# Up-projections as three 256-column products per weight block, with the modulated input moved 32 bytes against the weights

## The chip, the core and the metric

One core of a Trainium2 chip runs the whole kernel as one launch. The metric is the device time in microseconds. Three runs of the kernel before have a median of 2254.69 us (2251.78 to 2254.91). One more execution was taken by the hardware profiler; it took 2256.46 us, and its instructions span 2254.7 us.

## The reference

A trunk of two decoder layers over one sequence of 256 tokens, width 2048, all in float32. Layer 0 mixes tokens with a forgetting attention (16 heads of 128), layer 1 with a sliding-window attention (32 query heads of 64 in 4 groups, window 128, learned sinks). Each mixer is followed by a gated ConvFFN of inner width 5632. A conditioning vector `c` gives shift, scale and gate of every sub-layer:

```
c_act = silu(c)
for i in range(2):
    mod = c_act @ ada_w[i] + ada_b[i]                 # 2048 x 12288
    sh1, sc1, g1, sh2, sc2, g2 = split(mod, 6)
    h = x * (1 + sc1) + sh1
    y = attention_i(h)                                # fox_w_in / swa_w_in, then w_o
    x = layer_norm(ALPHA * x + (1 + g1) * y)
    h = x * (1 + sc2) + sh2
    u = h @ ffn_w_up[i]                               # 2048 x 11264
    u = u[s-2]*w0 + u[s-1]*w1 + u[s]*w2 + conv_b      # causal, along the tokens
    g, val = split(u, 2)
    y = (silu(g) * val) @ ffn_w_down[i]               # 5632 x 2048
    x = layer_norm(ALPHA * x + (1 + g2) * y)
```

## The kernel before, in words

**Products in three parts.** The large matrix products run on TensorE in the fp32r format. To keep float32 accuracy each operand is split into a high part (the value rounded to fp32r) and a low part (what is left). A product is then high·high + high·low + low·high, added up in PSUM. `stream` (L256 on) walks over a weight matrix in blocks of 256 rows by 512 columns: one DMA from the SP queue brings a block `w` (512 KB), ScalarE writes its high part `wh` (L264), VectorE its low part `wl` (L275), and then the block's products are issued by the function that the caller gave. `w` has 10 buffers, `wh` and `wl` 4 each. Every matmul instruction loads its own stationary operand (128 x 128) first.

**The modulated input.** `h` of a sub-layer lies transposed in SBUF, for each of 16 chunks of 128 features the 256 tokens of the high part and, right behind them, the 256 tokens of the low part. This is the tile `hHL`, [128, 16, 2, 256]; `hH` and `hL` are views of it.

**Two kinds of product.** Where the input is stationary and the weights move (`x_mm`, tiles named `xs`), each instruction has 512 moving columns. This is used for the value projections, the sliding-window layer's projections, both output projections and the down-projection, whose stationary operand is the gated activation `gT`. Where the weights are stationary (`w_mm`, tiles `ws`), each instruction moves 256 tokens; the q and k projections of layer 0 do this, in three products per 128 x 128 weight piece. The up-projections have a form of their own, `u_mm` (tiles `us`): two products per weight piece. The first moves all 512 columns of a chunk of `hHL` over the high weights, which leaves high·high in one half of a PSUM bank and low·high in the other; the second moves the 256 columns of `hH` over the low weights, into the first half.

**The up-projection pass.** `conv_ffn` splits the inner width into two parts (6 and 5 blocks of 512 columns). For each block it makes two passes of `w_stationary`, one for the gate half and one for the value half, each over all 16 chunks (8 weight blocks); then the down-projection of that part follows. A pass fills four banks of the eight in PSUM. What follows a pass is deferred: `evac` is a generator of which a step is run before each later weight block's products. Its `conv` adds the two halves of a bank (ScalarE copies the second half to SBUF at L1071, VectorE adds it at L1073), then does the convolution along the tokens (L1075 on ScalarE, L1076 and L1078 on VectorE).

**Work in the gaps.** The conditioning products (`ada_w`, 201 MB) run on VectorE as multiply-adds (L404), fed at a rate per weight block that `ada.update` sets. All pools are rings; the order on each engine is that of the program as the tile framework's scheduler lays it.

**Where tiles lie.** In the built program `hHL` starts at a multiple of 256 bytes in each partition. The weight buffers (`w`, `wh`, `wl`) and the general tiles of pool `gp` (`gT`, `oT`, `qh`, `kT`, `A`, ...) all start at 224 bytes beyond a multiple of 256.

Of the kernel before, what the change touches and what calls it, by code (L numbers as in the profile page):

```python
# [10 lines left out]
F32 = mybir.dt.float32  # L11
F32R = mybir.dt.float32r
I32 = mybir.dt.int32
AF = mybir.ActivationFunctionType
ALU = mybir.AluOpType
AX = mybir.AxisListType

P = 128
D = 2048
S = 256  # L20
NT = S // P
KC = D // P
# [19 lines left out]
def hybrid_trunk(ctx: ExitStack, tc: tile.TileContext, a: dict, out: bass.AP):  # L42
    nc = tc.nc
# [4 lines left out]
    cst = ctx.enter_context(tc.tile_pool(name="cst", bufs=1))  # L48
# [3 lines left out]
    tp = ctx.enter_context(tc.tile_pool(name="tp", bufs=4))  # L52
# [3 lines left out]
    def wtile(name="w"):  # L56
        return wp.tile([P, 2, WB], F32, tag="w", name=name)

    def gtile(name="g"):
        return gp.tile([P, 2, S], F32R, tag="g", name=name)  # L60

    def ttile(name="t"):
        return tp.tile([P, 2 * S], F32, tag="t", name=name)

    def bank(name="sm"):
        return psp.tile([P, 512], F32, tag="ps", name=name)

    def w_banks():
        return [bank("ws").rearrange("p (a s) -> p a s", a=2) for _ in range(2)]
# [4 lines left out]
    def mm(o, lhsT, rhs, start=False, stop=False, **kw):  # L74
        return nc.tensor.matmul(o, lhsT, rhs, start=start, stop=stop, **kw)  # L75

    def pin(ins, on=True):

        if on:
            tc.keep_in_program_order(ins)  # L80

    def split(h, l, src):

        nc.scalar.copy(h, src)  # L84
        nc.vector.tensor_tensor(l, src, f32(h), op=ALU.subtract)
# [125 lines left out]
    def then(fn, alone=False):  # L211

        if alone:
            lone.add(fn)
        work.append(fn)
        if len(work) == 1 and not ahead[0]:
            settle()
# [3 lines left out]
    def settle(left=0):  # L221
        while work and (ahead[0] > left or not left):
            f = work.pop(0)
            rest(f, *work)
            f()
# [17 lines left out]
    def defer(gen):  # L243

        post.append(gen)

    def run_post():
        for g in list(post):
            if next(g, post) is post:
                post.remove(g)  # L250
# [5 lines left out]
    def stream(wsrc, row0, col, ks, use):  # L256

        for kc in ks[::2]:
            r0 = (row0 + kc) * P
            w = wtile()  # L260
            pin(nc.sync.dma_start(w, wsrc[r0:r0 + 2 * P, col:col + WB].rearrange("(k p) f -> p k f", p=P)), False)
            h = hl.tile([P, 2, WB], F32R, tag="wh", name="wh")
            l = hl.tile([P, 2, WB], F32R, tag="wl", name="wl")
            pin(nc.scalar.copy(h, w), False)  # L264

            def go(kc=kc, h=h, l=l):
                ahead[0] -= 1
                run_post()
                use(kc, h, l)
                if feeds:  # L270
                    feeds.pop(0)()
                tick()

            def residual_(w=w, h=h, l=l, go=go):
                pin(nc.vector.tensor_tensor(l, w, f32(h), op=ALU.subtract), behind[0] > 0)  # L275
                behind[0] -= 1
                del residuals[go]

            ahead[0] += 1
            weights.add(go)  # L280
            residuals[go] = residual_
            work.append(go)
            settle(2)
# [25 lines left out]
    def w_mm(ps, kc, h, l, last=KC - 1, first=0):  # L309

        for i in range(2):
            for f in range(4):
                o = ps[f // 2][:, f % 2, :]
                wh, wl = h[:, i, f * P:(f + 1) * P], l[:, i, f * P:(f + 1) * P]
                mm(o, wh, hH[:, kc + i, :], start=kc + i == first and f % 2 == 0, skip_group_check=True)
                mm(o, wh, hL[:, kc + i, :], skip_group_check=True)
                mm(o, wl, hH[:, kc + i, :], stop=kc + i == last, skip_group_check=True)

    def u_banks():
        return [bank("us").rearrange("p (a s) -> p a s", a=2) for _ in range(4)]  # L320

    def u_mm(ps, kc, h, l):

        for f in range(4):
            for i in range(2):
                wh, wl = h[:, i, f * P:(f + 1) * P], l[:, i, f * P:(f + 1) * P]
                mm(ps[f], wh, hHL[:, kc + i], start=kc + i == 0, skip_group_check=True)
                mm(ps[f][:, 0, :], wl, hH[:, kc + i, :], stop=kc + i == KC - 1, skip_group_check=True)

    def x_stationary(wsrc, col, k0, nk, stat, end=0):  # L330

        ps = x_banks()
        use = x_mm_end(ps, stat, nk, end) if end else lambda kc, h, l: x_mm(ps, kc, h, l, stat, nk - 1)
        stream(wsrc, k0, col, list(range(nk)), use)
        return ps

    def w_stationary(wsrc, col):

        ps = u_banks()
        stream(wsrc, 0, col, list(range(KC)), lambda kc, h, l: u_mm(ps, kc, h, l))  # L340
        return ps


# [22 lines left out]
    def tick():  # L366
        ada_tick()
        if not feeds:
            step()
# [110 lines left out]
            ada_step()  # L480


    hHL = cst.tile([P, KC, 2, S], F32R, name="hHL")
    hH, hL = hHL[:, :, 0, :], hHL[:, :, 1, :]

    def mod_turn(k, n=1):

# [576 lines left out]
    def conv_ffn(l):  # L1064
        w_up, w_dn = a["ffn_w_up"][l], a["ffn_w_down"][l]
        NB = DFF // WB
        cw = lambda j, f: ccol[:, l, j, f:f + 1]

        def conv(pf, f):
            c = tp.tile([P, S], F32, tag="c", bufs=2, name="c")  # L1070
            nc.scalar.copy(c, pf[:, 1, :])  # L1071
            pf = pf[:, 0, :]
            nc.vector.tensor_tensor(pf, pf, c, op=ALU.add)  # L1073
            u = tp.tile([P, S], F32, tag="u", bufs=3, name="u")
            nc.scalar.activation(u, pf, AF.Identity, bias=cw(CW, f), scale=cw(2, f))  # L1075
            nc.vector.scalar_tensor_tensor(u[:, 1:], pf[:, :S - 1], cw(1, f), u[:, 1:],  # L1076
                                           op0=ALU.mult, op1=ALU.add)
            nc.vector.scalar_tensor_tensor(u[:, 2:], pf[:, :S - 2], cw(0, f), u[:, 2:],  # L1078
                                           op0=ALU.mult, op1=ALU.add)
            return u  # L1080

        def evac(ps, f0, then):
            u = None
            for f in range(5):
                v = conv(ps[f], f0 + f) if f < 4 else None
                if u is not None:
                    then(f - 1, u)
                u = v
                yield

        def silu(sil):
            def f_(f, u):
                nc.scalar.activation(sil[f // 2][:, (f % 2) * S:(f % 2 + 1) * S], u, AF.Silu)
            return f_

        def gated(sil, gT):
            def f_(f, u):
                nc.vector.tensor_tensor(u, u, sil[f // 2][:, (f % 2) * S:(f % 2 + 1) * S], op=ALU.mult)
                g = gtile("gT")
                split(g[:, 0, :], g[:, 1, :], u)  # L1100
                gT.append(g)
            return f_

        sbs = [(0, 6), (6, NB)]
        for si, (b0, b1) in enumerate(sbs):
            gT = []
            then(lambda: ada.update(rate=(0.64, 0.4)[l]))
            for b in range(b0, b1):
                ps = w_stationary(w_up, b * WB)
                sil = [ttile("sil") for _ in range(2)]  # L1110
                then(lambda ps=ps, b=b, sil=sil: defer(evac(ps, b * 4, silu(sil))))
                ps = w_stationary(w_up, DFF + b * WB)
                then(lambda ps=ps, b=b, sil=sil, gT=gT: defer(evac(ps, DFF // P + b * 4, gated(sil, gT))))

            def stat(kc, t, gT=gT):
                while kc >= len(gT):
                    run_post()
                return gT[kc][:, 0, t * P:(t + 1) * P], gT[kc][:, 1, t * P:(t + 1) * P]

            def ready(si=si):  # L1120
                if si == 0:
                    drain()
                ada_need(l, 5)
                ada["rate"] = (0.78, 0.4)[l]

            then(ready)
            for d in range(D // WB):
                ps = x_stationary(w_dn, d * WB, b0 * 4, (b1 - b0) * 4, stat, (2, 4)[l] if si > 0 and d == D // WB - 1 else 0)
                then(lambda ps=ps, d=d, si=si: defer(residual(ps, d, gates[l, 5], si == len(sbs) - 1)),
                     si > 0 and d == D // WB - 1)  # L1130
        then(lambda: (flush(), ada.update(gate_free=True)), True)
# [26 lines left out]
    for t in range(NT):  # L1158
        mu, rs, _ = moments[t]
        for d in range(D // 512):  # L1160
            c = slice(d * 512, (d + 1) * 512)
# [29 lines left out]
```

## Time and profile before

| What | Before |
|---|---|
| median of 3 runs | 2254.69 us (2251.78 to 2254.91) |
| profiled execution: its time, its span | 2256.46 us, 2254.7 us |
| TensorE matmul busy | 2203.7 us (98%), 12087 instructions recorded |
| TensorE weight load busy | 1908.6 us (85%) |
| VectorE busy | 1847.5 us (82%) |
| ScalarE busy | 1209.7 us (54%) |
| HBM | 602.66 MB, 267 GB/s on average |
| up-projection stages | 481 to 759, 892 to 1117, 1506 to 1780 and 1910 to 2132 us |

How to read it: matmuls are pipelined and the end of each is modelled, so the "busy" time of one (393 ns for a 512-column product) is longer than the step from its start to the next one's start. The step is what counts, and it is read from the start column of the timeline. In the timeline "x2" means that two equal instructions in a row were merged into one line, which carries the start of the first.

### The profile page before, as it was taken

To read this page: it belongs to the slowest core of one execution; us is meant where nothing else is said; L and a number is where in the kernel's file an instruction comes from. 1 tells how busy PE (TensorE), PEld (TensorE's weight loads), DVE (VectorE), ACT (ScalarE), POOL (GpSimd) and SP (SyncE) were. 2 spreads that over 40 slices of the span, in tenths; PEclk is the share of its full clock that TensorE was granted. 3 is DMA by queue.
4 is the path that set the end of the run, shared out by engine and by line. 5 is a ranking of instruction groups with operands and counts; after the bars stand their busy time and mean duration, and the time that the engine had idled before them with its cause. 6 is when DMAs were issued, how large, how long until landed. Compare 5 with 4: busy or idle time off the path is not lost. (4 is left out here: it accounts for less than half of the span.)

```text
span 2254.7 us, 33120 instructions
## 1 busy us (share of the span) xinstructions
PE 2203.7 (98%) x12087; PEld 1908.6 (85%) x12087; DVE 1847.5 (82%) x2626; ACT 1209.7 (54%) x2009; POOL 22.8 (1%) x52
## 2 busy tenths in 40 slices
PE   6999999999999999999999999999999999999997
PEld 5999888788888888888887788788888888888886
DVE  6879999979989978799888899769988655676766
ACT  3435655455555543655634588746555533555542
POOL 0000000000000000000000000000000000000000
PEclk9999999999999999999999999999999999999999
DMA  9999999958978989889887777557887555565553
GB/s 336 371 336 364 349 357 325 329 200 298 327 266 296 315 299 339 272 277 319 280 309 284 244 246 243 206 185 262 289 270 256 190 192 195 189 193 189 188 195 112
DMA packets 274228, 602.66 MB, mean 267 GB/s; under 512 B 21062, under 2 KB 29960, under 8 KB 273552
## 3 DMA queue, kind: packets, MB, share of 16 engines
q1 hardware_dynamic: 273008, 595.85, 76.5%
q0 software_dynamic: 1056, 4.69, 0.6%
q8 instruction: 94, 1.54, 0.3%
q14 instruction: 70, 0.57, 0.1%
HBM read 598.37 MB, written 2.10 MB: 266 GB/s over the span
## 5 line engine op out<-in xcount | busy, mean ns | idle before, releaser
L264 ACT CAST wh<-w 128x1024 fp32r<-128x1024 f32 x728 | 763.8, 1051 | 806.4 <-PE us L75 284.5
L275 DVE TENSOR_TENSOR wl<-w,wh 128x1024 fp32r<-128x1024 f32 x728 | 887.2, 1223 | 297.0 <-ACT wh L264 285.1
L75 PE MATMUL us<-hHL,wh 128*128 128x512 f32 x2816 | 983.7, 393 | 0.0
L75 PE MATMUL us<-hHL,wl 128*128 128x256 f32 x2816 | 790.4, 282 | 3.0 <-DVE wl L275 3.0
L75 PEld LDWEIGHTS us<-hHL,wh 128*128 128x128 f32 x2816 | 528.9, 188 | 112.0 <-issue 2.5
L75 PEld LDWEIGHTS us<-hHL,wl 128*128 128x128 f32 x2816 | 533.0, 189 | 8.4 <-DVE wl L275 4.3
L75 PE MATMUL xs<-wh,gT 128*128 128x512 f32 x1408 | 435.5, 390 | 0.0
L75 PEld LDWEIGHTS xs<-wh,gT 128*128 128x128 f32 x1408 | 264.3, 188 | 54.6
L75 PE MATMUL xs<-wl,gT 128*128 128x512 f32 x704 | 273.9, 389 | 0.0
L75 PE MATMUL xs<-wh,hHL 128*128 128x512 f32 x704 | 237.6, 403 | 0.1
L404 DVE SCALAR_TENSOR_TENSOR acc<-wa,cact,acc 128x1024 f32<-128x1024 f32 x180 | 228.8, 1280 | 0.0
L75 PE MATMUL ws<-hHL,wh 128*128 128x256 f32 x1024 | 191.3, 289 | 4.4 <-ACT hHL L84 2.1
L75 PEld LDWEIGHTS ws<-hHL,wh 128*128 128x128 f32 x1024 | 163.1, 196 | 6.9 <-ACT hHL L84 2.3
L404 DVE SCALAR_TENSOR_TENSOR acc<-wa,cactp,acc 128x1024 f32<-128x1024 f32 x128 | 162.6, 1281 | 0.0
L75 PEld LDWEIGHTS xs<-wh,hHL 128*128 128x128 f32 x704 | 131.5, 189 | 29.4 <-issue 1.0
L75 PEld LDWEIGHTS xs<-wl,gT 128*128 128x128 f32 x704 | 132.2, 188 | 27.3
L75 PE MATMUL ws<-hHL,wl 128*128 128x256 f32 x512 | 144.7, 290 | 2.2 <-DVE wl L275 2.2
L75 PE MATMUL xs<-wl,hHL 128*128 128x512 f32 x352 | 140.6, 400 | 1.6 <-DVE wl L275 1.5
L75 PE MATMUL xs<-wh,oT 128*128 128x512 f32 x384 | 124.6, 394 | 0.8 <-ACT wh L264 0.7
L1075 ACT ACTIVATE u<-us,ccol 128x256 f32<-128x256 f32 x176 | 98.0, 561 | 39.6 <-DVE us L1073 39.5
L75 PEld LDWEIGHTS ws<-hHL,wl 128*128 128x128 f32 x512 | 99.5, 197 | 2.8 <-DVE wl L275 2.8
L1076 DVE SCALAR_TENSOR_TENSOR u<-us,ccol,u 128x255 f32<-128x255 f32 x176 | 83.6, 480 | 13.2 <-ACT u L1075 12.9
(222 smaller groups left out, 1761.2 us busy)
## 6 DMA issues: line engine op xcount, KB each, us to landing
w<-in_ffn_w_up_dram SPq DMA_DIRECT2D x352, 512.0 KB, 4.6
wa<-in_ada_w_dram SPq DMA_DIRECT2D x320, 512.0 KB, 5.4
w<-in_ffn_w_down_dram SPq DMA_DIRECT2D x176, 512.0 KB, 4.1
w<-in_fox_w_in_dram SPq DMA_DIRECT2D x96, 512.0 KB, 7.0
wo<-in_ada_w_dram SPq DMA_DIRECT2D x48, 512.0 KB, 8.4
w<-in_swa_w_in_dram SPq DMA_DIRECT2D x40, 512.0 KB, 5.0
w<-in_fox_w_o_dram SPq DMA_DIRECT2D x32, 512.0 KB, 6.2
w<-in_swa_w_o_dram SPq DMA_DIRECT2D x32, 512.0 KB, 4.7
```

The costliest lines, as they stand in the source:

```text
L75: return nc.tensor.matmul(o, lhsT, rhs, start=start, stop=stop, **kw)
L264: pin(nc.scalar.copy(h, w), False)
L275: pin(nc.vector.tensor_tensor(l, w, f32(h), op=ALU.subtract), behind[0] > 0)
L404: pin(nc.vector.scalar_tensor_tensor(ac, wo, (cactp if row else cact)[:, k:k + 1], ac, op0=ALU.mult, op1=ALU.add), True)
L1075: nc.scalar.activation(u, pf, AF.Identity, bias=cw(CW, f), scale=cw(2, f))
L1076: nc.vector.scalar_tensor_tensor(u[:, 1:], pf[:, :S - 1], cw(1, f), u[:, 1:], op0=ALU.mult, op1=ALU.add)
```

## The change

It has four parts. The up-projections use `w_mm`, as the q and k projections of layer 0 do: per weight piece three products of 256 columns, two banks per pass in place of four. `conv` therefore reads finished sums, and the copy and the add go (L1071 to L1074). `evac` takes two steps per 128 columns in place of one. And the modulated input becomes two planes, all of `hH` and then all of `hL`, in a tile with 64 elements to spare, starting 8 elements (32 bytes) into it; the DMA scratch area at the bottom of SBUF is cut from 4096 to 2048 bytes. In the built program the planes now start at 32 bytes beyond a multiple of 256, and the weight buffers and general tiles at 224 as before, so these lie 192 bytes (mod 256) above the modulated input where they lay 224 above it.

```
-    def u_banks():
-        return [bank("us").rearrange("p (a s) -> p a s", a=2) for _ in range(4)]
-
-    def u_mm(ps, kc, h, l):
-        for f in range(4):
-            for i in range(2):
-                wh, wl = h[:, i, f * P:(f + 1) * P], l[:, i, f * P:(f + 1) * P]
-                mm(ps[f], wh, hHL[:, kc + i], start=kc + i == 0, skip_group_check=True)
-                mm(ps[f][:, 0, :], wl, hH[:, kc + i, :], stop=kc + i == KC - 1, skip_group_check=True)
...
     def w_stationary(wsrc, col):
-        ps = u_banks()
-        stream(wsrc, 0, col, list(range(KC)), lambda kc, h, l: u_mm(ps, kc, h, l))
+        ps = w_banks()
+        stream(wsrc, 0, col, list(range(KC)), lambda kc, h, l: w_mm(ps, kc, h, l))
         return ps
...
-    hHL = cst.tile([P, KC, 2, S], F32R, name="hHL")
-    hH, hL = hHL[:, :, 0, :], hHL[:, :, 1, :]
+    hpad = cst.tile([P, 2 * KC * S + 64], F32R, name="hH")
+    hH, hL = (hpad[:, 8 + a * KC * S:8 + (a + 1) * KC * S].rearrange("p (k s) -> p k s", s=S) for a in range(2))
...
         def conv(pf, f):
-            c = tp.tile([P, S], F32, tag="c", bufs=2, name="c")
-            nc.scalar.copy(c, pf[:, 1, :])
-            pf = pf[:, 0, :]
-            nc.vector.tensor_tensor(pf, pf, c, op=ALU.add)
             u = tp.tile([P, S], F32, tag="u", bufs=3, name="u")
...
-                v = conv(ps[f], f0 + f) if f < 4 else None
+                v = conv(ps[f // 2][:, f % 2, :], f0 + f) if f < 4 else None
                 if u is not None:
                     then(f - 1, u)
                 u = v
                 yield
+                yield
...
-    nc = _bacc.Bacc("TRN2", target_bir_lowering=False, num_devices=1, dynamic_dma_scratch_size=4096)
+    nc = _bacc.Bacc("TRN2", target_bir_lowering=False, num_devices=1, dynamic_dma_scratch_size=2048)
```

The first place is TensorE in the first weight block of the first up-projection pass. The number behind a tile's name tells buffers apart: `us_4824` and `us_4825` are the first two of the pass's four PSUM banks. Before:

```order
L75 MATMUL us_4824<-hHL_127,wh_4830 128x512
L75 MATMUL us_4824<-hHL_127,wl_4831 128x256
L75 MATMUL us_4824<-hHL_127,wh_4830 128x512
L75 MATMUL us_4824<-hHL_127,wl_4831 128x256
L75 MATMUL us_4825<-hHL_127,wh_4830 128x512
L75 MATMUL us_4825<-hHL_127,wl_4831 128x256
L75 MATMUL us_4825<-hHL_127,wh_4830 128x512
L75 MATMUL us_4825<-hHL_127,wl_4831 128x256
```

In the changed program, at the same weight block (`ws_4824` and `ws_4825` are all the banks that the pass has):

```order
L75 MATMUL ws_4824<-hH_127,wh_4828 128x256 x2
L75 MATMUL ws_4824<-hH_127,wl_4829 128x256
L75 MATMUL ws_4825<-hH_127,wh_4828 128x256
L75 MATMUL ws_4825<-hH_127,wl_4829 128x256
L75 MATMUL ws_4825<-hH_127,wh_4828 128x256 x2
L75 MATMUL ws_4825<-hH_127,wl_4829 128x256
L75 MATMUL ws_4824<-hH_127,wh_4828 128x256 x2
```

Each pair of a 512- and a 256-column product has become three of 256, with the high weights loaded twice in a row. A pass adds into half banks, and the block's first 128 rows go over all four column pieces before its second 128 rows do, where before the two row halves of one column piece followed each other.

The second place is VectorE at the end of the same pass, where the first bank is evacuated (`wl` is a weight block's low part, `u` the convolution's result, `x` the residual stream, `acc` the sum of a conditioning vector). Before:

```order
L275 TENSOR_TENSOR wl<-w,wh 128x1024
L673 TENSOR_SCALAR x<-ln,x 128x512
L1073 TENSOR_TENSOR us<-us,c 128x256
L275 TENSOR_TENSOR wl<-w,wh 128x1024
L1076 TENSOR_SCALAR u<-us,ccol,u 128x255
L1073 TENSOR_TENSOR us<-us,c 128x256
L1078 TENSOR_SCALAR u<-us,ccol,u 128x254
L404 TENSOR_SCALAR acc<-wa,cactp,acc 128x1024
```

Now:

```order
L275 TENSOR_TENSOR wl<-w,wh 128x1024
L662 TENSOR_SCALAR x<-ln,x 128x512
L1061 TENSOR_SCALAR u<-ws,ccol,u 128x255
L275 TENSOR_TENSOR wl<-w,wh 128x1024
L1063 TENSOR_SCALAR u<-ws,ccol,u 128x254
L393 TENSOR_SCALAR acc<-wa,cactp,acc 128x1024
```

The adds are gone, and the low parts of the weights stand with fewer instructions between them (lines have moved up by 11 to 15).

## The prediction

> **What bounds the kernel now.** I read the page's head first, then the groups by form, then busy time by stage, TensorE's waits, and last the timeline, because only starts give a matmul's true step.
>
> ```profile
> span 2254.7 us, 33120 instructions
> PE 2203.7 (98%) x12087; PEld 1908.6 (85%) x12087; DVE 1847.5 (82%) x2626; ACT 1209.7 (54%) x2009; POOL 22.8 (1%) x52
> ```
>
> TensorE is busy throughout. By stage (engines' busy us, granted clock, DMA share, GB/s):
>
> ```profile
> 60.00:190.00 130.00, 128.72 (x898) 120.71 (x898) 107.50 (x109) 55.70 (x71) 2.58 (x5) 0.95 1.02 358
> 190.00:350.00 160.00, 154.58 (x1118) 142.78 (x1116) 150.89 (x212) 91.58 (x179) 5.85 (x12) 1.00 0.99 354
> 480.00:760.00 280.00, 277.02 (x1575) 241.97 (x1574) 259.77 (x362) 160.47 (x249) 0.00 (x0) 0.99 0.84 288
> 892.00:1117.00 225.00, 225.00 (x1310) 199.77 (x1309) 198.19 (x273) 133.20 (x240) 0.00 (x0) 1.00 0.85 289
> 1506.00:1780.00 274.00, 274.00 (x1571) 240.92 (x1570) 236.67 (x337) 158.46 (x247) 0.00 (x0) 1.00 0.77 255
> 1910.00:2132.00 222.00, 222.00 (x1281) 196.73 (x1281) 152.82 (x226) 123.26 (x190) 0.00 (x0) 1.00 0.59 190
> ```
>
> The last four rows are the up-projections, 1001 of 2255 us: TensorE never pauses there, while DMA (0.59 to 0.85) and VectorE have room, VectorE least in the first (259.77 of 280). From 60 to 350 us the DMA engines are full (1.02, 0.99), so weights' arrival limits that stretch as much as products do. TensorE's waits in an up-projection, over the whole span:
>
> ```profile
> PE us L75 <- DVE wl L275: 3.0, 3, 1.4
> ```
>
> So what a weight piece's products take decides. The groups (busy us, mean ns with a modelled end):
>
> ```profile
> L75 PE MATMUL us<-hHL,wh 128*128 128x512 f32 x2816 | 983.7, 393 | 0.0
> L75 PE MATMUL us<-hHL,wl 128*128 128x256 f32 x2816 | 790.4, 282 | 3.0 <-DVE wl L275 3.0
> L75 PE MATMUL ws<-hHL,wh 128*128 128x256 f32 x1024 | 191.3, 289 | 4.4 <-ACT hHL L84 2.1 <-ACT wh L264 1.3 <-ACT hHL L503 1.0
> L75 PE MATMUL ws<-hHL,wl 128*128 128x256 f32 x512 | 144.7, 290 | 2.2 <-DVE wl L275 2.2
> L75 PE MATMUL xs<-wh,hHL 128*128 128x512 f32 x704 | 237.6, 403 | 0.1
> L75 PE MATMUL xs<-wl,hHL 128*128 128x512 f32 x352 | 140.6, 400 | 1.6 <-DVE wl L275 1.5
> ```
>
> The means overlap, so only their counts are used. In each timeline piece below the first and the last row of an unbroken run of products give its step.
>
> ```profile
> 599.70 0.39 PE L75 MATMUL us<-hHL,wh 128*128 128x512 f32 x1
> ...
> 605.94 0.39 PE L75 MATMUL us<-hHL,wh 128*128 128x512 f32 x1
> ```
>
> Between them lie 18 pairs of a 512- and a 256-column product: 6.24 us / 18 = 346.7 ns a pair.
>
> ```profile
> 275.39 0.40 PE L75 MATMUL ws<-hHL,wh 128*128 128x256 f32 x2
> ...
> 278.89 0.28 PE L75 MATMUL ws<-hHL,wh 128*128 128x256 f32 x1
> ```
>
> Ten triples, thirty products of just the kind that the change brings to the up-projection: 3.50 us / 30 = 116.7 ns, 350.0 a triple.
>
> **The change, part by part.** *The products.* 2816 pairs become triples. At 116.7 ns this would lose 2816 x 3.3 = 9.3 us, so the 32 bytes decide. The trace has three places of the stationary tile above the moving one (mod 256): 224 in the `ws` run, 0 where both are general tiles, 32 where the input is stationary and weights move. Place 0, 256 columns, in an attention score:
>
> ```profile
> 282.61 0.28 PE L75 MATMUL S<-qh 128*128 128x256 f32 x1
> ...
> 282.97 0.39 PE L75 MATMUL ws<-hHL,wh 128*128 128x256 f32 x2
> ```
>
> Three products in 0.36 us: 120 ns. Place 0, 512 columns (27 products), and place 32, 512 columns (12 products):
>
> ```profile
> 2149.85 0.62 PE L75 MATMUL xs<-wh,gT 128*128 128x512 f32 x2
> ...
> 2155.97 0.39 PE L75 MATMUL xs<-wh,gT 128*128 128x512 f32 x1
> ```
>
> ```profile
> 1369.92 0.39 PE L75 MATMUL xs<-wh,hHL 128*128 128x512 f32 x1
> ...
> 1372.71 0.81 PE L75 MATMUL o<-pT,V 128*128 128x256 f32 x4
> ```
>
> 6.12 / 27 = 226.7 ns and 2.79 / 12 = 232.5 ns. So products of one size differ by place, and from 32 to 0 to 224 each 32 bytes downward made them shorter: by 5.8 ns at 512 columns, by 3.3 at 256. The floor is what a product costs that moves next to nothing and only loads its weights:
>
> ```profile
> 472.16 3.63 PE L75 MATMUL sm<-ones,acc 128*128 128x1 f32 x32
> 475.65 0.42 PE L493 MATMUL sm<-ident,x 128*128 128x128 f32 x2
> ```
>
> 3.49 / 32 = 109 ns. No row shows place 192. Its bounds are 109 (the load's pace) and 120 (place 0); I take one more step of 3.3 down from 224, the nearest row: 113.4, a triple 340.1. Term: 2816 x (340.1 - 346.7) = **-18.6 us**, all on the path, since TensorE does not pause there.
>
> The rows put the place's effect at 3 to 6 ns a product. [...]
>
> *The other weight-stationary products.* The 1536 `ws` products get the same 3.3 ns: -5.1 us if all counts, 0 if the full DMA engines of 60 to 350 us merely make TensorE wait longer. Taken: **-2.5**.
>
> *The input as stationary operand.* 1056 `xs` products go from place 32 to 64. No row shows it: back to place 0's step would be 1056 x -5.8 = -6.1 us, a further step of the same slope +6.1. Taken: **0**, both ends kept.
>
> *VectorE and ScalarE.* 176 copies and 176 adds go:
>
> ```profile
> L1071 ACT COPY c<-us x176: 355/370/398, 506.2 to 2134.5; 128x256 f32<-128x256 f32 x176
> L1073 DVE TENSOR_TENSOR us<-us,c x176: 420/426/439, 510.4 to 2140.8; 128x256 f32<-128x256 f32 x176
> L1075 ACT ACTIVATE u<-us,ccol x176: 544/563/579, 511.3 to 2141.7; 128x256 f32<-128x256 f32 x176
> L1076 DVE SCALAR_TENSOR_TENSOR u<-us,ccol,u x176: 472/479/492, 511.9 to 2143.0; 128x255 f32<-128x255 f32 x176
> L1078 DVE SCALAR_TENSOR_TENSOR u<-us,ccol,u x176: 471/478/492, 512.6 to 2143.7; 128x254 f32<-128x254 f32 x176
> ```
>
> 176 x 0.370 = 65 us of ScalarE and 176 x 0.426 = 75 us of VectorE, all beside TensorE's products, which wait only the 3.0 us above. With 48 adds (20 us) out of the first up-projection, VectorE has 240 of some 272 us there, and the low weights come earlier: **-3.0**, that wait gone. Late next is TensorE itself.
>
> *Free of cost.* Four banks a pass become two, so no product can wait longer for a bank. The low weights are first needed after two 256-column products, 233 ns, where it was one of 512. The second `yield` spreads an evacuation over ten weight blocks, longer than the eight of a pass, but a down-projection after it needs the last `gT` only in its tenth or twelfth block; without that cover each of the four down-projections would stand for one convolution's chain, 563 + 479 + 478 ns by the rows above, 6 us in all. The 2816 more products and loads go out at the rate that the `ws` run already has. The scratch area changes no place mod 256.
>
> Sum: -18.6 - 2.5 + 0 - 3.0 = **-24.1 us** on a span of 2254.7, 2230.6. The profiled execution took 2256.46, 1.8 above its span, and the runs' median of 2254.69 is 1.8 below it; so the forecast for the median is **2230.6 us**.
>
> **The rivals.** *A, the load's pace.* At place 192 load and stream do not meet, and a product takes the 109 ns floor: 2816 x (327 - 346.7) = -55.5, `ws` half of 1536 x -7.7 = -5.9, the wait -3.0: -64, 2190 us; half-way there, 111 ns, 2205. For it speaks that the trend still falls at 224; against it that no fp32r run with 256 columns gets near.
>
> *B, the place is worth nothing* and the change therefore does not do what its padding says: triples at 350.0, +9.3 - 3.0 = +6.3, **2261 us, slower**. It decides from 115.6 ns a product upward. For it: the 5.8 and 3.3 ns come from different stages and neighbours, and 116.7 is only 3 ns off 120. [...]
>
> *C, the wrong way.* The places form a ring, so somewhere the step must rise again; if 192 is like place 0, 120 ns, triples cost 360: 2816 x 13.3 = +37.5, `ws` +5.1, without the wait -3.0: +39.6, 2294 us.
>
> **How the numbers follow.** Forecast 0.49, A 0.21, B 0.17, C 0.13. The range runs from 2198 (between A's two prices, leaving out some 0.06 of it) to 2265 (B with 4 us of the `xs` term on top); it leaves out C, 0.13. What a measurement of this kernel can tell from no change is about 0.2%, 4.5 us. Faster by more: forecast and A less 0.02 whose products stay near 115.5, 0.68. Within: that 0.02 and 0.04 of B, 0.06. Slower: 0.13 of B and C, 0.26.
>
> **What would show it.** Right: `ws` triples of about 340 ns in the up-projections, stages of some 261 us for the first part of a layer where 768 pairs took 266, no waits for `wl`, VectorE's busy time down by 75 us. `xs` products on the input away from 232.5 ns show the third term's sign. Wrong: triples at 350 (B) or 360 (C), or TensorE pauses in the up-projections that eat a shorter step, for low weights, banks or DMA.

## The result: 2268.7 us, slower, and the profile after

Three runs of the changed kernel take 2268.7 us in the median (2268.22 to 2270.11), against 2254.69 before: a ratio of 1.0063, 95% interval 1.0048 to 1.0077, so slower by 0.6 %, clear of the noise. The forecast was 2230.6 us, and the time lies above the range. The head of the profile after, span first, then each engine's busy time:

```profile
span 2266.9 us, 38317 instructions
PE 2218.6 (98%) x14903; PEld 2036.4 (90%) x14903; DVE 1795.4 (79%) x2450; ACT 1164.8 (51%) x1833; POOL 22.7 (1%) x52
```

2816 products and 2816 loads more, as forecast; VectorE's row falls by 52 us and ScalarE's by 45; the removed 176 adds of 0.426 us were 75, but a row counts instructions that overlap in the trace once, and they overlap less now: VectorE's single durations add up to 2017.8 us before and 1935.4 after, 170.3 and 140.0 above its row. The four up-projection stages, by busy us of each engine, granted clock, DMA share and GB/s:

```profile
478.00:757.00 279.00, 278.84 (x2335) 276.22 (x2334) 245.68 (x312) 146.49 (x201) 0.00 (x0) 1.00 0.85 292
890.00:1119.00 229.00, 229.00 (x1950) 229.00 (x1949) 188.09 (x235) 123.40 (x202) 0.00 (x0) 1.00 0.83 284
1509.00:1787.00 278.00, 278.00 (x2334) 275.76 (x2333) 222.13 (x290) 147.21 (x201) 0.00 (x0) 1.00 0.76 252
1918.00:2144.00 226.00, 226.00 (x1921) 226.00 (x1920) 140.94 (x188) 114.36 (x153) 0.00 (x0) 1.00 0.58 187
```

TensorE is busy for 1011.84 of these 1012 us; before, it was for 995.92 of the 998.9 us of its four stages. They are where the time went. From each stage's first product to the first product of the down-projection behind it:

| stage | before | after | difference |
|---|---|---|---|
| 1 | 480.8 to 759.2: 278.4 us | 478.0 to 757.4: 279.4 us | +1.0 |
| 2 | 891.7 to 1116.6: 224.9 | 889.9 to 1118.8: 228.9 | +4.0 |
| 3 | 1506.2 to 1779.9: 273.7 | 1508.7 to 1787.4: 278.7 | +5.0 |
| 4 | 1910.5 to 2132.4: 221.9 | 1918.0 to 2144.1: 226.1 | +4.2 |

Together +14.2 us; the medians lie 14.0 us apart. The timeline of the first stage has the new step; the run below holds 11 triples:

```profile
599.90 0.40 PE L75 MATMUL ws<-hH,wh 128*128 128x256 f32 x2
...
603.78 0.40 PE L75 MATMUL ws<-hH,wh 128*128 128x256 f32 x2
```

3.88 us / 33 = 117.6 ns a product, 352.7 a triple. The prediction needed 113.4 and 340.1, the pair before had 346.7.

### The profile page after: what moved, and what is told of

The parts are those of the page before. It is cut to its first block, busy times and chain, and to the rows that moved or that the text cites. A ratio compares the mean times of both kernels' runs of the same rounds, so it can differ in the third digit from the quotient of the medians.

```text
span 2266.9 us, 38317 instructions
## 1 busy us (share of the span) xinstructions
PE 2218.6 (98%) x14903; PEld 2036.4 (90%) x14903; DVE 1795.4 (79%) x2450; ACT 1164.8 (51%) x1833; POOL 22.7 (1%) x52
## 5 line engine op out<-in xcount | busy, mean ns | idle before, releaser
L75 PE MATMUL ws<-hH,wh 128*128 128x256 f32 x6656 | 1195.0, 282 | 4.5 <-ACT hH L84 2.1
L75 PEld LDWEIGHTS ws<-hH,wh 128*128 128x128 f32 x6656 | 1024.6, 189 | 12.5 <-issue 4.8
L75 PE MATMUL ws<-hH,wl 128*128 128x256 f32 x3328 | 930.2, 281 | 2.7 <-DVE wl L275 2.6
L75 PEld LDWEIGHTS ws<-hH,wl 128*128 128x128 f32 x3328 | 627.2, 189 | 3.7 <-DVE wl L275 3.5
L75 PE MATMUL xs<-wh,hH 128*128 128x512 f32 x704 | 236.9, 402 | 0.1
L75 PEld LDWEIGHTS xs<-wh,hH 128*128 128x128 f32 x704 | 131.0, 188 | 29.7 <-issue 1.0
L75 PE MATMUL xs<-wl,hH 128*128 128x512 f32 x352 | 140.5, 400 | 1.2 <-DVE wl L275 1.0
L1060 ACT ACTIVATE u<-ws,ccol 128x256 f32<-128x256 f32 x176 | 96.7, 561 | 57.3 <-PE ws L75 50.6
L1061 DVE SCALAR_TENSOR_TENSOR u<-ws,ccol,u 128x255 f32<-128x255 f32 x176 | 82.4, 476 | 20.1 <-ACT u L1060 20.0
L1063 DVE SCALAR_TENSOR_TENSOR u<-ws,ccol,u 128x254 f32<-128x254 f32 x176 | 82.9, 476 | 2.1
```

## The experiments

The first set kept everything and changed one thing each: the place (a kernel is named by its shape, triple or pair, and by the place of the weights above the input, mod 256; the changed kernel is the triple at 192, the one before the pair at 224). Two theories stood against each other: P, that the place sets the step, and S, that it is worth nothing. In every run the weights stay at 224 and only the input moves, so the runs do not separate the place of one operand against the other from the input's own place mod 256. The edit is one number:

```
-    hH, hL = (hpad[:, 8 + a * KC * S:8 + (a + 1) * KC * S] ...
+    hH, hL = (hpad[:, 0 + a * KC * S:0 + (a + 1) * KC * S] ...      # place 224
+    hH, hL = (hpad[:, 56 + a * KC * S:56 + (a + 1) * KC * S] ...    # place 0; 32: 96, 24: 128, 16: 160, 40: 64, 48: 32
```

**Triple at 224.** 

> The changed kernel with the planes starting at the tile's first byte, so that the weights lie 224 bytes (mod 256) above the input, as before the change. Theory P (the place sets a product's step, as the prediction had it, only with the sign of the last step wrong): 256-column products in the up-projections step at 116.7 ns as in the q and k projections before, a triple 350.0, and the kernel is 2816 x 3 x 1.0 = 8 us faster than the changed one, about 2260 us. Theory S (the step is set by the number of columns plus a fixed cost per product; the place is worth a nanosecond or less and 116.7 was the product of a mixed stage): 117.5 to 118, 2266 to 2269 us.

Measured: 2260.62 us (8 runs), ratio to the kernel before 1.0028 (1.0016 to 1.0039). In this and the following rows the fourth stage from 1930 to 2110 us is shown, restricted to the up-projection's tiles, so TensorE's busy time divided by the count of products is the step. A row also counts the two or three products that are still under way at its start, so this comes out 0.1 to 0.2 ns below the step read from starts.

```profile
1930.00:2110.00 180.00, 180.00 (x1545) 180.00 (x1544) 29.20 (x64) 17.51 (x32) 1.00 0.60 188
```

180 / 1545 = 116.5 ns. The same row of the changed kernel itself, at 192:

```profile
1930.00:2110.00 180.00, 180.00 (x1531) 180.00 (x1530) 29.21 (x64) 17.53 (x32) 1.00 0.59 187
```

117.6 ns. The third stage of the triple at 224 is not like its fourth:

```profile
1530.00:1760.00 230.00, 229.71 (x1948) 229.28 (x1947) 37.48 (x81) 22.57 (x41) 1.00 0.81 268
```

By starts it has 117.7 ns, as the changed kernel has in all stages, where the other three stages at 224 have 116.7. So the 32 bytes are worth 1.1 ns a product in three stages of four in this trace, and about 8 us in the medians, in the direction opposite to the one forecast, and the triples alone lose 6 us against the pairs.

**Pair at 192, the padding alone.** 

> The kernel before with the input moved by 32 bytes alone: pairs of 512 and 256 columns as before, the scratch area cut to 2048 bytes, place 192 for the weights. Theory P: the pair, 346.7 ns at place 224, becomes longer by 1 to 2 ns as the triples' products did, 2816 x 1.5 = 4 us slower than before, about 2259 us. Theory S: 346 to 347 ns a pair, 2252 to 2257 us.

```
-    hHL = cst.tile([P, KC, 2, S], F32R, name="hHL")
+    hpad = cst.tile([P, 2 * KC * S + 64], F32R, name="hHL")
+    hHL = hpad[:, 8:8 + 2 * KC * S].rearrange("p (k a s) -> p k a s", a=2, s=S)
```

Measured: 2268.13 us, ratio 1.0058 (1.0045 to 1.0072). The padding, with the scratch area cut as in the change, costs the old shape 13 us, more than forecast by either theory; its stages are 281.6, 228.4, 276.2 and 223.3 us long, and by starts its pairs step at 352.9, 352.3, 349.5 and 348.9 ns in them. The two parts of the change therefore don't add up: shape alone +6, padding alone +13, both +14 us; the padding costs pairs 13 us and triples 8.

**Triple at 0.** 

> The changed kernel with the input 224 bytes into its tile, so that weights and input lie at the same place mod 256. Theory P, from the attention score's 120 ns at that place: triples of 360 ns in the up-projections, 2816 x 6.9 = 19 us slower than the changed kernel, 2288 us. Theory S: 117 to 118.5 ns a product, 2265 to 2272 us.

```profile
1930.00:2110.00 180.00, 179.31 (x1495) 179.49 (x1496) 25.47 (x56) 15.33 (x28) 1.00 0.58 183
```

Measured: 2285.68 us in one run. This stage begins 0.7 us into the window; 179.31 us over 1495 products are 119.9 ns. The attention score's 120 ns at that place did carry over. The theory that the place is worth nothing had 2265 to 2272 us here, and is dead.

**Triples at 96, 160, 128, 64 and 32: the rest of the ring.** 

> The changed kernel with the input 128 bytes into its tile: weights 96 bytes (mod 256) above it, a place that no earlier trace has. Theory P gives a step different from that at 224, 192 and 0 by some ns, of unknown sign, between 109 (the load's pace) and 125 ns. Theory S: 117 to 118.5 ns, 2265 to 2272 us.

> The changed kernel with the input 64 bytes into its tile, weights 160 bytes (mod 256) above it. Known so far: place 0 120.0, 224 116.9, 192 117.7, 96 118.0 ns a product. Theory P, with a smooth ring: 117.7 to 118.5 ns, 2266 to 2275 us. Were there a hidden good place, it would show as under 116 ns.

> The changed kernel with the input 96 bytes into its tile, weights 128 bytes (mod 256) above it, the far side of the ring. Smooth ring: 117.5 to 118.5 ns, 2266 to 2275 us. A good place: under 116 ns, below 2255 us.

> The changed kernel with the input 160 bytes into its tile, weights 64 bytes (mod 256) above it. Smooth ring between 96 (118.0 ns) and 0 (120.0 ns): 118 to 119.5 ns, 2270 to 2282 us.

> The last place of the ring for triples, weights 32 bytes (mod 256) above the input. Known: 0 120.0, 64 114.7 (113.3 or 117.8), 96 118.0, 128 119.2, 160 120.0, 192 117.7, 224 116.9 ns. The ring is no smooth curve, so no more than 113 to 120 ns can be expected, 2235 to 2286 us.

Measured, one run each but where said:

| place above the input | up-projection step, ns | time, us |
|---|---|---|
| 0 | 120.0 | 2285.7 |
| 32 | 118.3 | 2274.3 |
| 64 | 113.3 or 117.6 | 2243.0 |
| 96 | 118.0 | 2272.5 |
| 128 | 119.2 | 2279.4 |
| 160 | 120.0 | 2288.9 |
| 192 | 117.7 | 2268.7 (3 runs) |
| 224 | 116.9 | 2260.6 (8 runs) |

(The step is the mean, over all four stages of one execution, of the time between the starts of neighbouring products, long gaps left out; at 64 the two values that occur. At three more places the stages of that execution differ: 116.7 to 117.7 ns at 224, 117.4 to 118.7 at 96, 118.7 to 120.0 at 128.) Two valleys, at 64 and 224, two peaks, at 0 and 160; with one trace for most places, small differences between neighbours are not shown. The good place exists, but it is 64, the mirror image of the 192 that the change chose. 2243.0 us is the first time below the kernel before.

**Triple at 64, timed.** 

> The same kernel as tri_64, timed. In its first trace the products of the up-projections stepped at 113.3 ns in three stages and at 117.8 in the fourth, from the first weight block to the last, with nothing else different. If the step has two states and each stage falls into one of them by chance, the times of single runs should lie apart by up to 2816/4 x 3 x 4.5 = 9 us a stage, between 2234 and 2270 us; if the state is set by the program, all runs lie at 2241 to 2245 us. Theory S is dead either way.

Measured: 2249.74 us in the median of 12 runs, 2240.41 to 2259.81, ratio 0.9974 (0.9956 to 0.9992). The spread of 19 us is more than twice that of the kernel before in the same series (8 us, 2249.05 to 2257.29). Two traces of this one kernel, part of the third and of the fourth stage, the earlier execution first (they are from two chips, but the 12 runs on the second chip spread by 19 us by themselves):

```profile
1530.00:1730.00 200.00, 200.00 (x1767) 200.00 (x1766) 35.38 (x76) 20.30 (x37) 1.00 0.86 284
1930.00:2110.00 180.00, 180.00 (x1531) 180.00 (x1530) 29.22 (x64) 17.53 (x32) 1.00 0.64 187
```

```profile
1530.00:1730.00 200.00, 200.00 (x1701) 200.00 (x1700) 34.60 (x74) 20.25 (x37) 1.00 0.83 272
1930.00:2110.00 180.00, 180.00 (x1530) 180.00 (x1530) 29.23 (x64) 17.50 (x32) 1.00 0.64 187
```

The third stage runs at 200 / 1767 = 113.2 ns in one execution and at 200 / 1701 = 117.6 in the other, with the same instructions and the same granted clock (1.00). The step has two states, and each held here for some 1700 products. By starts they are 113.3 and 117.8 ns, and the long one is the step of the changed kernel at 192.

**Pairs at 64 and at 0.** 

> The kernel before (pairs, copies and adds kept) with the input 160 bytes into its tile, weights 64 bytes (mod 256) above it: the place alone, without the change of shape. [...] If place 64 is good for triples only: 345 to 352 ns, 2250 to 2270 us.

> The kernel before with weights at the same place as the input (mod 256). Triples are worst there (120.0 ns). Theory P for the pair: 352 to 360 ns, 2268 to 2292 us; but products with a stationary input and the general tiles, at place 0 among themselves, had 226.7 ns for 512 columns, 2 less than the pair's own at 224, so 344 ns (2245 us) would say that place 0 is good for 512 columns and bad for 256.

Measured: 2269.63 us, ratio 1.0073 (1.0060 to 1.0085), at 64, and 2272.6 at 0 (one run). The fourth stage of the pair at 224 (the kernel before), at 64 and at 0, 180 us over half the count:

```profile
1930.00:2110.00 180.00, 180.00 (x1040) 159.59 (x1040) 41.95 (x97) 29.30 (x66) 1.00 0.59 190
```

```profile
1930.00:2110.00 180.00, 180.00 (x1021) 156.34 (x1020) 39.88 (x92) 27.59 (x63) 1.00 0.64 186
```

```profile
1930.00:2110.00 180.00, 180.00 (x1020) 155.98 (x1019) 39.86 (x92) 27.48 (x63) 1.00 0.64 186
```

346.2, 352.6 and 352.9 ns. The pair at 192 lies between, at 348.9 to 352.9 by starts. What is best for triples is bad for pairs: the 512-column half steps at 235 ns at place 64 where it had 228 at 224. The kernel before lay at the best of the four places tried for its shape. A place cannot be judged apart from the shape that uses it.

**Pushing the state: transposes between the products.** In the traces of the triple at 64, long stretches of the short step began behind a group of 128-column transposes:

```profile
929.62 0.28 PE L75 MATMUL ws<-hH,wl 128*128 128x256 f32 x1
929.74 0.60 PE L431 MATMUL sm<-ident,acc 128*128 128x128 f32 x4
930.10 0.48 PE L75 MATMUL ws<-hH,wh 128*128 128x256 f32 x2
```

```profile
905.00:925.00 20.00, 20.00 (x172) 20.00 (x171) 3.17 (x7) 1.68 (x3) 1.00 0.91 309
950.00:970.00 20.00, 20.00 (x179) 20.00 (x179) 3.66 (x8) 2.24 (x4) 1.00 0.83 276
```

Ahead of it 20 us hold 172 products, behind it 179. In a window this short the two or three products under way at its start weigh 1.5 ns; by starts the steps are 117.8 and 113.3. Two kernels put such transposes in on purpose, a third does so at 192:

```
+    def kick(n=4):
+        o = bank("kick")
+        for j in range(n):
+            pin(nc.tensor.transpose(o[:, j * P:(j + 1) * P], ident, ident))
...
+        def use(kc, h, l):
+            w_mm(ps, kc, h, l)
+            if kc in kicks:
+                kick()
```

> The changed kernel at place 64 with four 128-column transposes of the identity, whose result nobody reads, after the third and the sixth weight block of the first pass of each up-projection stage: 8 groups, 8 x 0.45 = 3.6 us of TensorE. In the traces of tri_64 the long stretches of 113.3 ns began right behind such groups of transposes (930 us) and the stage without any (from 1892 us) stayed at 117.8. Theory K (the state is set by what stands between the products): all four stages at 113.3 ns, stages 3 and 4 of about 270 and 219 us, 2234 to 2243 us in every run. Theory R (the state is drawn at random at the start of a stage): no change, 2240 to 2263 us, runs 20 us apart.

> The same place with one transpose after the third weight block of every pass: 44 x 0.11 = 4.8 us of TensorE. Theory K with any fp32 transpose enough: 2234 to 2243 us, runs within 6 us; if one transpose is too short to set the state: 2245 to 2265 us. Theory R: 2245 to 2265 us.

> The changed kernel as it was (place 192) with the eight groups of four transposes. If place 192 can hold 113.3 ns once it has been set: stages 2 to 4 at 113.3 ns, 2240 us. If, as in its own trace, the state falls back within one or two weight blocks there: 117.8 ns but for 8 x 48 products, 2266 to 2275 us.

Measured: four transposes twice a stage, 2243.55 us in the median of 12 runs, 2234.95 to 2256.72, ratio 0.9951 (0.9932 to 0.9969). One transpose in every pass, 2249.36 us in 6 runs, 2247.03 to 2249.86, ratio 0.9971 (0.9959 to 0.9982). At 192, 2274.86 us. In the trace of the groups of four (2256.72 us, the longest of its 12 runs) the fourth and the third stage have these rows:

```profile
1935.00:2110.00 175.00, 175.00 (x1546) 175.00 (x1545) 29.17 (x64) 17.66 (x33) 1.00 0.67 194
1535.00:1735.00 200.00, 200.00 (x1701) 200.00 (x1700) 33.51 (x72) 19.23 (x35) 1.00 0.83 274
```

Stages 2 and 4 step at 113.5 ns, stages 1 and 3 at 117.3 and 117.7, so theory K, all four short in every run, is wrong. The trace of the single transposes shows what they do. Five windows of 20 us, each between two of them, and the second of them itself:

```profile
964.00:984.00 20.00, 20.00 (x179) 20.00 (x179) 1.91 (x4) 1.58 (x3) 1.00 0.88 290
985.50:1005.50 20.00, 20.00 (x172) 20.00 (x171) 3.84 (x9) 2.24 (x4) 1.00 0.88 302
1008.50:1028.50 20.00, 20.00 (x179) 20.00 (x179) 3.36 (x8) 2.15 (x4) 1.00 0.95 335
1030.00:1050.00 20.00, 20.00 (x172) 20.00 (x171) 3.73 (x8) 2.25 (x4) 1.00 0.90 304
1053.00:1073.00 20.00, 20.00 (x178) 20.00 (x178) 2.87 (x6) 2.08 (x4) 1.00 0.92 312
```

```profile
984.44 0.28 PE L75 MATMUL ws<-hH,wl 128*128 128x256 f32 x1
984.56 0.27 PE L330 MATMUL kick<-ident 128*128 128x128 f32 x1
984.59 0.48 PE L75 MATMUL ws<-hH,wh 128*128 128x256 f32 x2
```

The state can change at a transpose, and it then holds to the next one: 179, 172, 179, 172 and 178 products. Of the 44 transposes of this execution 37 stand among up-projection products alone. By starts, the short step followed the long one in 13 of 13 cases; behind the short one it stayed in 13 and turned long in 11. So a transpose does not choose the good state, as theory K would have it, nor is the state drawn only at a stage's start, as theory R would: here it changed at interruptions, and at the lone transposes it left the long state every time; in between it was mostly kept. Once the step changed at a wait of the products. In the first stage of the kernel with groups of four, TensorE waited 0.8 us for a low weight, at 528 us, with no transpose near; the rows are the wait, then the products before and behind it:

```profile
PE ws L75 <- DVE wl L275: 0.8, 1, 0.8
510.00:527.00 17.00, 17.00 (x152) 17.00 (x152) 2.31 (x5) 1.69 (x3) 1.00 0.94 327
530.00:547.00 17.00, 17.00 (x146) 17.00 (x146) 3.37 (x8) 1.59 (x3) 1.00 1.00 368
```

By starts that is 113.3 ns before and 117.8 behind. With 44 transposes an execution the runs lie within 3 us of each other; with few, 20 us apart. At 192 the fourth stage, behind the same groups of four, has this row:

```profile
1930.00:2110.00 180.00, 179.62 (x1523) 179.25 (x1523) 27.79 (x61) 16.92 (x31) 1.00 0.65 186
```

179.62 / 1523 = 117.9 ns. The 113.3 ns step occurs at 192 as well, for 48 products between two groups of transposes (942.3 to 947.9 us of this run), but it does not last there. What differs inside a product between the two steps, and what decides a draw, no run shows.

**The removed copies and adds.** 

> The changed kernel with the ScalarE copy and the VectorE operation put back before each convolution, on finished sums (the maximum of a value with itself, so the result stays): 176 x 0.37 us of ScalarE and 176 x 0.43 us of VectorE. If their removal gave the first up-projection stage its 4 us, the stage is 283 us instead of 279.4, the other three unchanged at 228.9, 278.7 and 226.1, and the kernel takes 2270 to 2275 us. If VectorE was cover throughout: 279 us, 2266 to 2270 us.

```
         def conv(pf, f):
+            c = tp.tile([P, S], F32, tag="c", bufs=2, name="c")
+            nc.scalar.copy(c, pf)
+            nc.vector.tensor_tensor(pf, pf, c, op=ALU.max)
```

The first two stages of this kernel:

```profile
480.00:763.00 283.00, 280.34 (x2336) 277.65 (x2335) 259.02 (x356) 158.92 (x245) 0.00 (x0) 0.99 0.86 286
896.00:1125.00 229.00, 229.00 (x1949) 228.97 (x1948) 199.53 (x271) 132.66 (x238) 0.00 (x0) 1.00 0.86 284
```

Measured: 2274.36 us; the first stage is 283.2 us long instead of 279.4, the other three are 228.9, 278.7 and 226.1, unchanged to a tenth. VectorE has 259 of 283 us there again, as before the change. TensorE's only wait of that stage is back with it:

```profile
PE ws L75 <- DVE wl L275: 2.6, 1, 2.6
```

The removal is worth 3.8 us by one execution each, in the stage where VectorE is fullest and nowhere else; 2.6 of it are this wait for a low weight.

**The load's pace.** 

> The changed kernel in which the up-projections' products move 128 tokens instead of 256 in all chunks but the first and the last, so the last 128 tokens' sums lack 14 of 16 chunks; loads, places and order stay. Theory L (the weight load's own pace sets the 117.7 ns): the step stays at 110 to 118 ns and the kernel at 2240 to 2270 us. Theory M (the moving stream sets it, 256 columns plus a cost per product): the load's pace of the one-column products, 112 ns, becomes the floor for 14 of 16 chunks, so it cannot fall below 112; a step of 112 would mean that load and stream were within 6 ns of each other all along and that no place could have won more than 17 us per 2816 triples. A step under 100 ns would mean that the floor in the prediction, 109 ns, was no floor.

This execution was granted a clock of 0.589 in the mean, and 0.63 already from 60 to 190 us, where it runs the same instructions as the changed kernel, which had 0.97 there; 3475.01 us and its steps say nothing about the edit. 

> The same kernel as half (128 moving tokens in 14 of 16 chunks of the up-projections, so sums of the last 128 tokens lack those chunks). If the low clock came from that execution: clock 0.99, and the products with 128 columns step at the load's pace, 108 to 113 ns, 2225 to 2250 us. If the kernel causes it: clock 0.6 again and some 3470 us.

Measured: 2239.13 us at a clock of 0.985, on another chip, so the kernel alone does not cause the low clock; what did is open. The fourth stage:

```profile
1930.00:2110.00 180.00, 180.00 (x1604) 180.00 (x1603) 29.22 (x64) 17.57 (x32) 1.00 0.64 197
```

180 / 1604 = 112.2 ns, with one product in eight still of 256 columns; the 128-column ones alone step at 111.4. Half the columns save only 6 ns (111.4 against 117.7), so something that does not shrink with the columns takes some 111 ns a product, and the short state of 113.3 is within 2 ns of it. That this is the load of the next weights fits the one-column products, which step at 111 to 112 ns, but another cost per product is not excluded.

## Why the prediction was wrong, point by point

**The step that failed** is the value taken for the unknown place: "I take one more step of 3.3 down from 224, the nearest row: 113.4". Three places were taken for a slope, one of them, 32, read at 512 columns only. At 256 columns there is no such slope: 32 has 118.3 ns and lies below the 120.0 of place 0. The ring has two valleys, 224 was the bottom of one, and 192 lies 1.1 ns up its other side. The term of -18.6 us became some +18: 2816 x (353.1 - 346.7), with 353.1 = 3 x 117.7. With the -3.8 below, that gives the +14 that was measured.

**The rows were right that the place counts.** That the place of the weights above the input changes a product's step was read from 226.7 against 232.5 ns, and eight places now show 113.3 to 120.0 at 256 columns, up to 6.7 ns a product; what makes the difference no run shows. Rival B took the place to be worth nothing and gave 2261 us, which the triple at 224 (2260.6) meets for another reason, namely that it kept the old place.

**Rival C** ("somewhere the step must rise again") was the right kind: right sign, with 353 ns a triple instead of its 360. The prediction had three points of a ring and no reason to prefer a neighbour's continuation to a turn.

**The floor held,** and lies higher than was read. No 48 up-projection products of 256 columns in a row stepped below 113.3. The 109 of the one-column row is a mean with one first start of 26 ns in it; the other 31 are 111 to 112, as the 111.4 of the 128-column products. Rival A's 2190 us would have needed 109; its half-way price of 111 ns was reached at none of the eight places either. That price was also summed too low: by the terms of the first price, 111 ns gives -38.6 for the products, -4.4 for half of the `ws` products and -3.0, so 2209 us and not 2205.

**The -3.0 us for VectorE** was right, in size and in mechanism: -3.8 by the kernel with the operations put back, 2.6 of it one wait for a low weight. The changed kernel's profile lists no wait of TensorE in its first up-projection stage; its whole trace has these for low weights of `ws` tiles, all in layer 0's q and k projections:

```profile
PE ws L75 <- DVE wl L275: 2.6, 3, 1.4
```

**The `ws` term, -2.5,** had the wrong sign, as the step had. What it was worth can't be seen: the up-projection starts at 478.0 us where it had started at 480.8, though those products got longer by 0.7 ns; two executions of the triple at 64 differ by 2.1 us in that start as well (478.5 and 476.4). From 60 to 350 us the DMA share is 1.01, after 1.00 before; that the weights' arrival sets this stretch is a reading of that share, which no run tested.

**The `xs` term, 0,** was right. Its group of 704 products, busy and mean:

```profile
L75 PE MATMUL xs<-wh,hH 128*128 128x512 f32 x704 | 236.9, 402 | 0.1
```

Before it had 237.6 and 403; by starts these products have 233.3 ns after 233.0, and the stretch from the end of stage 2 to the start of stage 3, which holds all products of the sliding-window layer, takes 389.9 us after 389.6.

**The things taken as free were free:** no wait for a bank or a `gT` appeared, and the stretches from stage 1 to 2 and from 3 to 4, each a down-projection, are 132.5 and 130.6 us long, as before.

## What to carry to other kernels

In the up-projections TensorE was busy for 1011.84 of 1012 us, and 6.4 ns more in a triple's step than in a pair's (353.1 against 346.7) were some 18 us of time: where it is never idle, read the step from starts, and read it for the same shape at the same relative place of the two operands. The place of an operand mod 256 bytes cost up to 6 % of a product here (113.3 against 120.0 ns), the best place differs between shapes (64 for triples, 113.3 or 117.6 ns; 224 of the four tried for pairs, 346.7 ns a pair), and it is no slope to be continued: eight cheap runs of one edit tell more than three rows of a trace. If one kernel's runs spread more than its neighbour's, look for stages that run in one of two steps; here a median from three runs would have told little.

## What the runs showed of the hardware that was not expected

The step of one and the same instruction stream has two states, 113.3 and 117.8 ns by starts at place 64; in one execution the short one held for all 1767 products of a 200 us row, the long one for the 1920 of a whole stage. It changed at single 128-column transposes between products, the long step turning short at all 13 that met it and the short one long at 11 of 24, and once at a wait of 0.8 us. The fastest kernel found, the triple at 64 with eight groups of four transposes, takes 2243.55 us in the median, 0.5 % less than the kernel before, though its interval (0.9932 to 0.9969) overlaps that of the triple at 64 without them (0.9956 to 0.9992). Its shortest run took 2235; all four stages in the short state at once would explain such a run, but no trace was taken of it. And one of the nineteen profiled executions here was granted 0.589 of TensorE's clock in the mean, and took 3475.01 us, where the same kernel took 2239.13 the next time.
